# Dense attention scores: the 64-row products of two pairs of key tiles in the two halves of the array's rows

## The chip, the cores and the metric

The kernel runs on one core of one Trainium2 chip. The metric is device time in microseconds (us), lower is better; the median of three runs of the kernel before is 1220.64 us (1220.6 to 1221.4).

## The reference

One encoder layer over 1024 positions of width 1024, all in float32: RMS norm, one projection, two attention mixers side by side, an output projection, and a gated MLP with a three-wide convolution. The change lies in the first mixer, dense attention with 8 query heads and 2 key/value heads of width 64:

```python
def global_gqa_attention(q, k, v):
    ...
    def block(qb):
        sc = jnp.einsum('bqkgd,bskd->bkgqs', qb, k, preferred_element_type=jnp.float32) * scale
        p = jax.nn.softmax(sc, axis=-1)
        return jnp.einsum('bkgqs,bskd->bqkgd', p.astype(v.dtype), v)
```

## The kernel before

To keep float32 accuracy, operands are split into a high part of a shorter float and a low rest, and a product is the sum of three products: high by high, high by low, low by high. The head width is 64, and TensorE contracts over 128 rows, so the scores of one key tile take two matmuls. The arrays have the contraction on the rows (partitions):

- `q2` (`R_Q2A`, two buffers by the group's parity): rows 0 to 63 the high part of four heads' queries, rows 64 to 127 the low part; 512 columns.
- `R_K2A`: rows 0 to 63 the low part of the keys, rows 64 to 127 the high part. By `q2` it gives low by high plus high by low in one matmul (L773).
- `R_KHA`: rows 0 to 63 the high part of the keys, copied there by a DMA; rows 64 to 127 zero. By `q2` it gives high by high (L774), with half of the rows multiplying zeros.

The work is cut into 16 groups `g` (a block of 128 query positions by the four heads of one key/value head). `a_main_bounded` runs over four pairs `j` of key tiles; a pair is 2 tiles of 128 keys and fills two PSUM banks: 0 and 1 for even `j`, 2 and 3 for odd. For each pair TensorE does four score matmuls, ScalarE (ACT) takes the exponential of the two banks (L779) into one of three buffers, ACT (VectorE, that is DVE, for `j` = 1) makes the high part of it (L783, L781), and DVE the low part (L784). Three pairs later `pv` (L757) multiplies with the values, six matmuls a pair. At the end of a group DVE copies the sum out of PSUM (L767), TensorE transposes it (L762), and DVE divides (L803, L804).

Between these runs side work: `a_prep(g + 1)` prepares the next group's queries: `nat` splits them (L665 on ACT, L666 on DVE), `first` transposes them on TensorE (L192) and copies them to `q2` (L687 on ACT). The tuple `plan` tells at which key tile `kt` (two in each pair) the next of these steps is taken. Norm and rotary work of the late query heads (L530 and the eight L304 on GpSimd, that is POOL; some on DVE) and the first head of the second mixer (`b_split`, `b_prep`) are dealt out in the same way.

A scheduler takes the program in the order written and sets each engine's own order, by its estimate of when operands are ready; engines run their own list in order. POOL's list holds tensor operations and POOL's DMAs in one line. After the stage comes the second, dilated mixer, whose first score matmuls (L986) follow directly.

Of the kernel before, what the change touches and what calls it, by code (L numbers as in the profile page):

```python
# [45 lines left out]
R_K2A = 16384  # L46
R_KHA = R_K2A + 2048
R_W = R_KHA + 6144
# [26 lines left out]
R_QLN = R_XT + 1024  # L75
R_Q2A = R_XT + 2048
R_QLA = R_XT + 3072
R_PH = R_XT + 4096
R_PL = R_XT + 6144
R_VB = R_XT + 8192  # L80
# [56 lines left out]
def tile_encoder_layer(ctx, tc, x, w_in, gains, outg, norm1_g, norm2_g, w_out, w_up, conv_w, conv_b,  # L137
# [14 lines left out]
    def emit(bounded):  # L152
# [3 lines left out]
        gp = nc.gpsimd  # L156
        mm = nc.tensor.matmul
# [5 lines left out]
        def r(off, n):  # L163
            return bigr[:, off:off + n]
# [20 lines left out]
        def bank(i, n=512, o=0):  # L185
            return PS[:, 512 * i + o:512 * i + o + n]
# [485 lines left out]
        def a_prep(g):  # L672
            b, kv = grp(g)
            o = 512 * (g % 2)
            q2 = R_Q2A + 512 * (g % 2)
            ql = R_QLA + 512 * (g % 2)

            def nat():
                if bounded:
                    return q_pair(qab(b) + 256 * kv, 64, vec, 4, o)  # L680
                q_nat(qab(b) + 256 * kv, 64, vec, 4, o)

            def first():
                t = next_tr()
                for i in range(4):
                    tr_r(t, i, r(R_QD + o + 128 * i, 128))
                act(r(q2, 512), bank(t), AF.Copy)  # L687

            def mx(i):
                for hf in range(2):  # L690
                    b = hf
                    mm(bank(b), r(q2 + 128 * i, 128), r(R_K2A + 1024 * kv + 512 * hf, 512), start=True, stop=True)
                    vec.tensor_reduce(f(SM_MC + 8 * hf + i, 1), bank(b), axis=AX.X, op=OP.max)

            def last():
                vec.tensor_tensor(rp(R_QLN + 512 * kv + 64, [128, 4]), f(SM_MC, 4), f(SM_MC + 8, 4), op=OP.max)
                t = next_tr()
                for i in range(4):
                    tr_r(t, i, r(R_QLN + 128 * (4 * kv + i), 128))
                act(r(ql, 512), bank(t), AF.Copy)  # L700

            if bounded:
                return [nat, first]
            return [nat, first] + [lambda i=i: mx(i) for i in range(4)] + [last]
# [38 lines left out]
        def a_main_bounded(g, prep, tail, late, plan, late_plan):  # L743

            b, kv = grp(g)
            b2, kv2 = grp(max(g - 2, 0))
            q2 = R_Q2A + 512 * (g % 2)
            ob = 6 + g % 2
            slots = {}

            def pv(j):
                ph, pl = slots[j]
                for u in range(2):
                    kt = 2 * j + u
                    v = R_VA + 132 * kt + 66 * kv
                    for i, (w, p) in enumerate(((v, ph), (v + 1056, ph), (v, pl))):
                        mm(bank(ob)[0:66], r(w, 66), r(p + 512 * u, 512), start=(kt == 0 and i == 0), stop=(kt == 7 and i == 2))  # L757

            def o_turn():
                t = next_tr()  # L760
                for i in range(4):
                    nc.tensor.transpose(bank(t, 66, 128 * i), f(F_OT + 128 * i, 128)[0:66], f(O_IDF, 66)[0:66])  # L762
                o_norm(t, 128, qab(b) + 256 * kv, ([64, 4], [1, 64]))

            def last():
                pv(3)
                vec.tensor_copy(f(F_OT, 512)[0:66], bank(ob)[0:66])  # L767

            for j in range(4):
                st = 2 * (j % 2)  # L770
                for u in range(2):
                    kt = 2 * j + u
                    mm(bank(st + u), r(R_K2A + 1024 * kv + 128 * kt, 128), r(q2, 512), start=True, stop=False)  # L773
                    mm(bank(st + u), r(R_KHA + 1024 * kv + 128 * kt, 128), r(q2, 512), start=False, stop=True)  # L774
                n = pairs[0]
                pairs[0] += 1
                p, ph, pl = F_PB[n % 3], R_PHB[j], R_PLB[j]
                slots[j] = ph, pl
                act(f(p, 1024), bank(st, 1024), AF.Exp)  # L779
                if j == 1:  # L780
                    vec.tensor_copy(r(ph, 1024), f(p, 1024))  # L781
                else:
                    act(r(ph, 1024), f(p, 1024), AF.Copy)  # L783
                vec.tensor_tensor(r(pl, 1024), f(p, 1024), rf(ph, 1024), op=OP.subtract)  # L784
                for kt in (2 * j, 2 * j + 1):
                    take(prep, plan[kt])
                    take(late, late_plan[kt])
                    now = f(qab(b2) + 256 * kv2, 1) if 0 < kt < 7 and g > 1 else \
                        rf(R_Q2A + 512 * ((g + (kt == 7)) % 2), 1)
                    for step in spread.pop((g, kt), []):  # L790
                        step(now)
                step = tail.pop(0) if tail else None
                if step:
                    step()
                if j > 2:
                    pv(j - 3)

            behind, turn[:] = turn[:], [o_turn]
            return [lambda: [t() for t in [lambda: pv(1)] + behind], lambda: pv(2), last, o_turn if g == 15 else None]
# [550 lines left out]
        for g in range(16):  # L1350

            prep += a_prep(g + 1) if g < 15 else []
            if g == 14:
                prep += [lambda: b_split(0)] + sum(sum(b_prep(0), []), [])
            plan = {14: (1, 1, 0, 1, 0, 1, 1, 0), 15: (1, 1, 0, 1, 0, 0, 0, 0)}.get(g, (0, 1, 0, 0, 1, 0, 0, 0)) if bounded else {14: (1, 1, 1, 1, 1, 2, 2, 2), 15: (2, 2, 2, 2, 1, 1, 1, 1)}.get(
                g, (1, 1, 1, 1, 1, 1, 1, 0))
            tail = a_main(g, prep, tail, late, plan, (0, 2, 2, 2, 1, 1, 1, 1))
            if g == 7:
                if not bounded:
                    dma(f(F_CNT, 384), cnt)  # L1360
                if not bounded:
                    gp.memset(fp(F_VCN + 64, [66, 8]), 1.0)
                    load_vc(0)
            if g in (4, 7):
                wo_load(g // 7)
            if g == 9:
                load_tee(0, 0)
                load_tee(0, 1)
                load_tmx(1)
            if g == 11:  # L1370
                load_k(0)
            if g == 13:
                load_k(1)
            if g == 10 and bounded:
                load_v(0)
            if g == (12 if bounded else 5):
                v_split(R_VB, F_VBN)
                load_v(1)
            if g > 3 and fills:
                b, kv = grp(g - 2 if bounded else g - 1)  # L1380
                fills.pop(0)(qab(b) + 256 * kv)
# [411 lines left out]
        for m in range(2, len(order)):  # L1793
            j, n = order[m]
# [111 lines left out]
```

## Time and profile before

| what | value |
|---|---|
| median of the runs | 1220.64 us |
| the profiled execution, its own time | 1221.38 us |
| span of its trace | 1219.6 us |
| the stage of dense attention (16 groups), in the trace | 207.5 to 364.8 us |
| score matmuls in it (L773 and L774) | 128 and 128 |
| pairs of key tiles (16 groups of 4) | 64 |

Times inside the trace are counted from the start of the span. PE is TensorE's matmul row, PEld its weight loads. A matmul's row starts when it is issued and its end is modelled, so that rows of back-to-back matmuls overlap: what one costs in a stream is the distance from start to start. In a table by windows the columns are the window, its length, the busy time of PE, PEld, DVE, ACT and POOL with the number of instructions, the granted TensorE clock (1.00 is full), the share of DMA and GB/s.

### The profile page before, as it was taken

How to read it: one execution, taken by the hardware profiler on the slowest of the kernel's cores; microseconds unless marked ns; L12 is line 12 of the kernel's file. 1: busy time of each engine (PE TensorE's matmuls, PEld its weight loads, DVE VectorE, ACT ScalarE, POOL GpSimd, SP SyncE). 2: the span in 40 equal slices, each digit the busy share in tenths (PEclk: the TensorE clock that was granted, in tenths of full speed). 3: DMA queues.
4: the chain of work that ended last, by engine and by line, in shares of the span. 5: the costliest groups of instructions: out<-in, count | busy, mean ns of one | idle time of the engine just before them, and what ended most of it. 6: DMA issues, size and time to landing. Idle time of an engine off the chain costs nothing.

```text
span 1219.6 us, 17814 instructions
## 1 busy us (share of the span) xinstructions
PE 1191.7 (98%) x6615; PEld 1007.2 (83%) x6615; DVE 998.0 (82%) x1324; ACT 674.1 (55%) x976; POOL 398.4 (33%) x307
## 2 busy tenths in 40 slices
PE   7999999999999999999999999999999999999998
PEld 7999999666669997888788888877888788888886
DVE  5988687989988878666999999999999997876673
ACT  7856455889887767436544444445444453543431
POOL 1710122230024530010465666557575644000000
PEclk9999999999999999999999999999999999999999
DMA  8036301020015655232132232322332257977872
GB/s 281 25 103 154 108 18 42 1 57 18 1 30 125 153 117 173 89 102 95 61 112 95 87 113 97 111 95 87 113 112 100 83 184 252 338 239 243 291 233 85
DMA packets 121565, 147.00 MB, mean 121 GB/s; under 512 B 51137, under 2 KB 79617, under 8 KB 121473
## 3 DMA queue, kind: packets, MB, share of 16 engines
q1 hardware_dynamic: 119329, 140.05, 35.9%
q0 software_dynamic: 2144, 5.77, 2.2%
q8 instruction: 53, 0.87, 0.3%
q14 instruction: 39, 0.32, 0.1%
HBM read 107.25 MB, written 33.82 MB: 116 GB/s over the span
## 4 chain that ended last, share of the span: by engine, by line
PE 68%; DVE 17%; issue 5%; ACT 4%; DMA 3%; POOL 1%; SPq 0%; DVEq 0%; ACTq 0%; POOLq 0%
DVE bigf L1603 7%; PE ps L1570 7%; PE ps L1572 6%; PE ps L1571 6%; PE ps L757 6%; PE ps L1704 6%; PE ps L1703 6%; PE ps L1702 6%; DVE bigf L1574 3%; PE ps L1125 2%; PE ps L1126 2%; PE ps L1124 2%; PE ps L434 2%; PE ps L435 2%; PE ps L773 2%
## 5 line engine op out<-in xcount | busy, mean ns | idle before, releaser
L1570 PE MATMUL ps<-bigr 128*128 128x512 f32 x616 | 241.0, 392 | 6.3 <-DVE bigf L1574 5.8
L1571 PE MATMUL ps<-bigr 128*128 128x512 f32 x616 | 239.7, 389 | 0.0
L1572 PE MATMUL ps<-bigr 128*128 128x512 f32 x616 | 239.7, 389 | 0.0
L1603 DVE SCALAR_TENSOR_TENSOR bigf<-bigf 128x768 f32<-128x768 f32 (+1 forms) x176 | 178.7, 1073 | 26.5 <-ACT bigf L1601 26.4
L1553 ACT ACTIVATE bigr<-bigf 128x512 fp32r<-128x512 f32 x154 | 93.2, 625 | 139.5 <-POOL bigf L1545 70.2
L1682 ACT ACTIVATE bigr<-bigf 128x1024 fp32r<-128x1024 f32 (+1 forms) x99 | 83.7, 867 | 115.8 <-PE ps L1704 67.6
L1570 PEld LDWEIGHTS ps<-bigr 128*128 128x128 f32 x616 | 115.6, 188 | 35.0 <-DVE bigf L1574 9.2
L1572 PEld LDWEIGHTS ps<-bigr 128*128 128x128 f32 x616 | 115.6, 188 | 24.1
L1571 PEld LDWEIGHTS ps<-bigr 128*128 128x128 f32 x616 | 115.7, 188 | 23.7
L434 PE MATMUL ps<-bigr 128*128 128x256 f32 x448 | 127.3, 285 | 1.2 <-ACT bigf L310 1.2
L1554 DVE TENSOR_TENSOR bigr<-bigf,bigr 128x512 fp32r<-128x512 f32 x112 | 125.2, 1135 | 3.2 <-ACT bigr L1553 2.5
L435 PE MATMUL ps<-bigr 128*128 128x256 f32 x448 | 126.9, 283 | 0.6 <-DVE bigr L418 0.6
L436 PE MATMUL ps<-bigr 128*128 128x256 f32 x448 | 126.7, 283 | 0.0
L1702 PE MATMUL ps<-bigr 128*128 128x512 f32 x308 | 119.8, 389 | 0.0
L1703 PE MATMUL ps<-bigr 128*128 128x512 f32 x308 | 119.8, 389 | 0.0
L1704 PE MATMUL ps<-bigr 128*128 128x512 f32 x308 | 119.8, 389 | 0.0
L1683 DVE TENSOR_TENSOR bigr<-bigf,bigr 128x1024 fp32r<-128x1024 f32 (+1 forms) x99 | 97.6, 1005 | 24.8 <-ACT bigr L1682 21.4
L757 PE MATMUL ps<-bigr 128*66 128x512 f32 x384 | 99.9, 394 | 0.0
L434 PEld LDWEIGHTS ps<-bigr 128*128 128x128 f32 x448 | 85.8, 192 | 1.8 <-ACT bigf L310 1.5
L435 PEld LDWEIGHTS ps<-bigr 128*128 128x128 f32 x448 | 85.9, 192 | 0.8 <-DVE bigr L418 0.8
L784 DVE TENSOR_TENSOR bigr<-bigf,bigr 128x1024 fp32r<-128x1024 f32 x64 | 80.8, 1269 | 6.4 <-ACT bigr L783 5.7
L436 PEld LDWEIGHTS ps<-bigr 128*128 128x128 f32 x448 | 85.9, 192 | 0.0
(231 smaller groups left out, 2508.8 us busy)
## 6 DMA issues: line engine op xcount, KB each, us to landing
bigf<-w_down SPq DMA_DIRECT2D x99, 256.0 KB, 4.3
bigf<-w_up SPq DMA_DIRECT2D x44, 512.0 KB, 3.6
bigf<-gscr SPq DMA_DIRECT2D x77, 256.0 KB, 4.3
gscr<-bigf SPq DMA_DIRECT2D x31, 512.0 KB, 2.6
bigf<-w_in SPq DMA_DIRECT2D x8, 1024.0 KB, 5.4
bigf<-x SPq DMA_DIRECT2D x15, 512.0 KB, 7.0
bigf<-w_out SPq DMA_DIRECT2D x8, 512.0 KB, 3.9
bigr<-bigr POOLq DMA_DIRECT2D x16, 256.0 KB, 3.8
```

Source lines behind the costliest of these rows:

```text
L434: mm(o, ah, wh, start=(k == 0 and t % 2 == 0 and n != 2), stop=False, skip_group_check=True)
L435: mm(o, ah, wl, start=False, stop=False, skip_group_check=True)
L436: mm(o, al, wh, start=False, stop=(k == 3), skip_group_check=True)
L757: mm(bank(ob)[0:66], r(w, 66), r(p + 512 * u, 512), start=(kt == 0 and i == 0), stop=(kt == 7 and i == 2))
L1554: (gp if n in (2, 4) and m > 3 else vec).tensor_tensor(rp(o + 512, [128, 4], [1, 128]), src, rfp(o, [128, 4], [1, 128]), op=OP.subtract)
L1570: mm(bank(b), wh, th, start=(k == 0 and n in (1, 5, 6, 7)), stop=False, skip_group_check=True)
L1571: mm(bank(b), wh, tl, start=False, stop=False, skip_group_check=True)
L1572: mm(bank(b), wl, th, start=False, stop=(k == 3), skip_group_check=True)
L1603: vec.scalar_tensor_tensor(f(a + o, n), f(i + d, n), w_, f(a + o, n), op0=OP.mult, op1=OP.add)
L1702: mm(o, ah, r(d, 512), start=(q == 0 and n in (1, 5, 2)), stop=False, skip_group_check=True)
L1703: mm(o, ah, r(d + 1024, 512), start=False, stop=False, skip_group_check=True)
L1704: mm(o, al, r(d, 512), start=False, stop=(q == NQ - 1), skip_group_check=True)
```

## The change

Every pair still takes its two L773 matmuls over 128 rows. The high-by-high products, which need 64 rows only, become 64-row matmuls: for the first key tile of a pair from rows 0 to 63 (`R_KHA` by `q2`), for the second from rows 64 to 127 (the high keys in the lower half of `R_K2A`, by a copy of the high queries at rows 64 to 127, `R_Q3A`). They write two different banks. So that two pairs' 64-row matmuls stand together, those of pair `j` (even) and pair `j + 1` are both issued at pair `j`: there they are the last products into pair `j`'s banks and the first ones into pair `j + 1`'s, to which the 128-row matmuls are added later. The copy `R_Q3A` is made for each group by a DMA on POOL's queue (64 rows by 512 columns, 128 KB), after the query copy. The tuple `plan` takes the query preparation one pair earlier.

```diff
+R_Q3A = R_W + 6144
...
                 act(r(q2, 512), bank(t), AF.Copy)
+                if bounded:
+                    gp.dma_start(r(R_Q3A + 512 * (g % 2), 512)[64:128], r(q2, 512)[0:64])
...
                 for u in range(2):
-                    kt = 2 * j + u
-                    mm(bank(st + u), r(R_K2A + 1024 * kv + 128 * kt, 128), r(q2, 512), start=True, stop=False)
-                    mm(bank(st + u), r(R_KHA + 1024 * kv + 128 * kt, 128), r(q2, 512), start=False, stop=True)
+                    mm(bank(st + u), r(R_K2A + 1024 * kv + 256 * j + 128 * u, 128), r(q2, 512), start=j % 2 == 0, stop=j % 2 == 1)
+                for i in (j, j + 1) if j % 2 == 0 else ():
+                    k2, kh = [o + 1024 * kv + 256 * i for o in (R_K2A, R_KHA)]
+                    for lo, k, q in ((0, kh, q2), (64, k2 + 128, R_Q3A + 512 * (g % 2))):
+                        mm(bank(2 * (i % 2) + lo // 64), r(k, 128)[lo:lo + 64], r(q, 512)[lo:lo + 64], start=i != j, stop=i == j)
...
-            plan = {14: (1, 1, 0, 1, 0, 1, 1, 0), 15: (1, 1, 0, 1, 0, 0, 0, 0)}.get(g, (0, 1, 0, 0, 1, 0, 0, 0)) if bounded else ...
+            plan = {14: (1, 0, 1, 0, 1, 1, 1, 0), 15: (1, 1, 0, 1, 0, 0, 0, 0)}.get(g, (0, 1, 1, 0, 0, 0, 0, 0)) if bounded else ...
```

Lines below L690 stand five further down in the changed kernel: L773 is L775, the 64-row matmuls are L779, L757 is L760, L192 is L193, L687 is L688, the new DMA is L690, L779 (the exponential) is L784, L783 is L788, L530 and L304 are L531 and L305, L838 is L843.

TensorE's list in the middle of a group, before. Two pairs of four score matmuls, with the next group's query transposes (L192) and the six value matmuls (L757) between them:

```order
L773 MATMUL ps<-bigr 128x512 [waits Activation_49]
L774 MATMUL ps<-bigr 128x512
L773 MATMUL ps<-bigr 128x512
L774 MATMUL ps<-bigr 128x512
L192 MATMUL ps<-bigr 128x128 x4
L757 MATMUL ps<-bigr 66x512 x2
L757 MATMUL ps<-bigr 66x512 [waits DVE_49]
L757 MATMUL ps<-bigr 66x512 x3
L773 MATMUL ps<-bigr 128x512 [waits Activation_49]
```

And with the change, an odd pair and the even one after it:

```order
L775 MATMUL ps<-bigr 128x512 x2
L193 MATMUL ps<-bigr 128x128 x4
L760 MATMUL ps<-bigr 66x512 x2
L760 MATMUL ps<-bigr 66x512 [waits DVE_49]
L760 MATMUL ps<-bigr 66x512 x3
L775 MATMUL ps<-bigr 128x512 [waits Activation_49]
L775 MATMUL ps<-bigr 128x512
L779 MATMUL ps<-bigr 128x512 x2
L779 MATMUL ps<-bigr 128x512 [waits Activation_49]
L779 MATMUL ps<-bigr 128x512
L760 MATMUL ps<-bigr 66x512 x2
```

The odd pair has two score matmuls left; the even one has two over 128 rows and then four over 64, and the third of these, which opens the next pair's banks, waits for ACT's exponential of the pair before. There are 128 matmuls L779 in the stage, in 35 unbroken stretches.

POOL's list in groups 0 to 4, before:

```order
L304 TENSOR_TENSOR bigf<-bigf 128x8x16 x5
L530 TENSOR_TENSOR bigf<-bigf 128x512 [waits DVE_49,Pool_49]
L304 TENSOR_TENSOR bigf<-bigf 128x8x16 [waits Pool_49]
L304 TENSOR_TENSOR bigf<-bigf 128x8x16 x7
L530 TENSOR_TENSOR bigf<-bigf 128x512 [waits DVE_49,Pool_49]
L304 TENSOR_TENSOR bigf<-bigf 128x8x16 [waits Pool_49]
L304 TENSOR_TENSOR bigf<-bigf 128x8x16 x7
L1452 MEMSET bigf 128x8
```

And with the change:

```order
L305 TENSOR_TENSOR bigf<-bigf 128x8x16 x5
L690 DMA bigr<-bigr 64x512 [waits Activation_49]
L690 DMA bigr<-bigr 64x512 [waits DMASW4_49,Activation_49]
L690 DMA bigr<-bigr 64x512 [waits DMASW5_49,Activation_49]
L531 TENSOR_TENSOR bigf<-bigf 128x512 [waits DVE_49,Pool_49]
L305 TENSOR_TENSOR bigf<-bigf 128x8x16 [waits Pool_49]
L305 TENSOR_TENSOR bigf<-bigf 128x8x16 x7
L690 DMA bigr<-bigr 64x512 [waits DMASW6_49,DMASW0_49,Activation_49]
L531 TENSOR_TENSOR bigf<-bigf 128x512 [waits DVE_49,Pool_49]
L305 TENSOR_TENSOR bigf<-bigf 128x8x16 [waits Pool_49]
L305 TENSOR_TENSOR bigf<-bigf 128x8x16 x7
L1457 MEMSET bigf 128x8
```

The copies of the queries of groups 1 to 3 stand ahead of the second rotary batch, that of group 4 between the second and the third, and that of group 5 behind the third and the MEMSET.

ACT's list around the second GpSimd split (L838), before, with one query copy (L687):

```order
L779 ACTIVATE bigf<-ps 128x1024 [waits DVE_49,PE_49] x2
L687 ACTIVATE bigr<-ps 128x512 [waits PE_49]
L783 ACTIVATE bigr<-bigf 128x1024 [waits Activation_49]
L838 ACTIVATE bigr<-bigf 128x8x64 [waits DMAHW6_49,DMAHW5_49,DMAHW7_49,DMAHW4_49,PE_49]
L779 ACTIVATE bigf<-ps 128x1024 [waits DVE_49,PE_49]
```

And with the change:

```order
L784 ACTIVATE bigf<-ps 128x1024 [waits DVE_49,PE_49]
L688 ACTIVATE bigr<-ps 128x512 [waits DMASW7_49,PE_49]
L784 ACTIVATE bigf<-ps 128x1024 [waits DVE_49,PE_49]
L788 ACTIVATE bigr<-bigf 128x1024 [waits Activation_49]
L843 ACTIVATE bigr<-bigf 128x8x64 [waits DMAHW6_49,DMAHW5_49,DMAHW7_49,DMAHW4_49,PE_49]
L784 ACTIVATE bigf<-ps 128x1024 [waits DVE_49,PE_49]
```

The query copy stands one exponential earlier, and waits for an earlier one of the new DMAs as well, which read the same buffer.

More of the change, by code (lines that the diff above doesn't have):

```diff
@@ L1354, in emit @@
                 prep += [lambda: b_split(0)] + sum(sum(b_prep(0), []), [])
-            plan = {14: (1, 1, 0, 1, 0, 1, 1, 0), 15: (1, 1, 0, 1, 0, 0, 0, 0)}.get(g, (0, 1, 0, 0, 1, 0, 0, 0)) if bounded else {14: (1, 1, 1, 1, 1, 2, 2, 2), 15: (2, 2, 2, 2, 1, 1, 1, 1)}.get(
+            plan = {14: (1, 0, 1, 0, 1, 1, 1, 0), 15: (1, 1, 0, 1, 0, 0, 0, 0)}.get(g, (0, 1, 1, 0, 0, 0, 0, 0)) if bounded else {14: (1, 1, 1, 1, 1, 2, 2, 2), 15: (2, 2, 2, 2, 1, 1, 1, 1)}.get(
                 g, (1, 1, 1, 1, 1, 1, 1, 0))
```

## Prediction

> **What bounds the kernel now.** I read the page's busy times first, then the chain of waits, then the stage of dense attention by windows of one group each, then the rows of single matmuls. The page:
>
> ```profile
> span 1219.6 us, 17814 instructions
> PE 1191.7 (98%) x6615; PEld 1007.2 (83%) x6615; DVE 998.0 (82%) x1324; ACT 674.1 (55%) x976; POOL 398.4 (33%) x307
> PE 68%; DVE 17%; issue 5%; ACT 4%; DMA 3%; POOL 1%; SPq 0%; DVEq 0%; ACTq 0%; POOLq 0%
> ```
>
> Over the whole span TensorE is the bound, and the chain that ended last runs 68% through it. But an average says nothing of one stage. Here are the 16 groups, a window each (columns: window, length, busy PE, PEld, DVE, ACT, POOL, clock, DMA share, GB/s):
>
> ```profile
> 207.50:213.00 5.50, 5.24 (x28) 3.93 (x26) 3.89 (x5) 4.66 (x7) 0.00 (x0) 1.00 0.00 0
> 213.00:223.30 10.30, 10.29 (x44) 6.94 (x45) 10.30 (x13) 9.55 (x12) 0.00 (x0) 1.00 0.00 0
> 223.30:233.20 9.90, 9.90 (x50) 6.87 (x49) 8.49 (x14) 8.02 (x11) 4.11 (x4) 1.00 0.01 2
> 233.20:243.00 9.80, 9.80 (x50) 6.80 (x48) 9.24 (x13) 7.82 (x10) 3.65 (x6) 1.00 0.00 1
> 243.00:252.90 9.90, 9.90 (x50) 6.88 (x49) 7.39 (x14) 7.92 (x10) 7.25 (x10) 1.00 0.19 47
> 252.90:264.20 11.30, 10.00 (x49) 6.73 (x48) 10.61 (x16) 8.38 (x11) 3.10 (x1) 1.00 0.36 88
> 264.20:274.10 9.90, 9.90 (x50) 6.89 (x49) 9.42 (x17) 9.26 (x13) 1.39 (x1) 1.00 0.11 27
> 274.10:283.90 9.80, 9.80 (x49) 6.72 (x48) 9.74 (x16) 9.70 (x12) 0.00 (x0) 1.00 0.19 54
> 283.90:293.80 9.90, 9.90 (x50) 6.89 (x50) 9.60 (x19) 8.78 (x11) 0.00 (x0) 1.00 0.01 2
> 293.80:303.90 10.10, 10.10 (x51) 6.77 (x49) 9.53 (x15) 9.50 (x13) 0.00 (x0) 1.00 0.00 0
> 303.90:313.60 9.70, 9.70 (x48) 6.81 (x48) 8.90 (x16) 9.66 (x12) 0.00 (x0) 1.00 0.01 2
> 313.60:323.50 9.90, 9.90 (x50) 6.86 (x49) 9.62 (x17) 8.06 (x10) 0.00 (x0) 1.00 0.00 1
> 323.50:333.30 9.80, 9.80 (x49) 6.80 (x48) 9.56 (x15) 7.83 (x9) 0.00 (x0) 1.00 0.00 0
> 333.30:343.10 9.80, 9.80 (x49) 6.86 (x48) 9.70 (x18) 8.30 (x12) 0.00 (x0) 1.00 0.13 28
> 343.10:354.70 11.60, 10.75 (x58) 7.49 (x57) 8.71 (x13) 10.05 (x14) 1.42 (x1) 1.00 0.00 1
> 354.70:364.80 10.10, 10.10 (x54) 7.15 (x53) 7.63 (x8) 9.60 (x14) 4.68 (x5) 1.00 0.27 54
> ```
>
> PE is busy without a gap in most groups, at the full clock. But DVE is close behind: 9.74 of 9.80 us in group 7 (the eighth row), all of group 1, over 95% in most of groups 7 to 13; ACT is at 9.70 and 9.66 in groups 7 and 10. So what TensorE saves in a group comes out only as far as the busier of the other two allows. The stage is 157.3 us (first to last window), and the dilated stage follows on PE at once, so a shift here reaches the end.
>
> The price of a matmul is read from start to start:
>
> ```profile
> 264.24 0.40 PE L773 MATMUL ps<-bigr 128*128 128x512 f32 x1
> 264.24 0.19 PEld L774 LDWEIGHTS ps<-bigr 128*128 128x128 f32 x1
> 264.47 0.39 PE L774 MATMUL ps<-bigr 128*128 128x512 f32 x1
> 264.70 0.39 PE L773 MATMUL ps<-bigr 128*128 128x512 f32 x1
> 264.93 0.40 PE L774 MATMUL ps<-bigr 128*128 128x512 f32 x1
> 265.16 1.54 PE L757 MATMUL ps<-bigr 128*66 128x512 f32 x6
> 266.54 0.41 PE L762 MATMUL ps<-bigf 66*128 66x66 f32 x4
> 266.75 0.48 PE L773 MATMUL ps<-bigr 128*128 128x512 f32 x1
> 267.07 0.39 PE L774 MATMUL ps<-bigr 128*128 128x512 f32 x1
> 270.04 0.46 PE L192 MATMUL ps<-bigr 128*128 128x128 f32 x4
> 270.34 1.59 PE L757 MATMUL ps<-bigr 128*66 128x512 f32 x6
> ```
>
> 0.23 us each, and the six of L757 take 1.38. The weights of the next matmul load while one streams (the PEld row starts with it). The row's length, 0.39, is 0.16 more than 0.23: the modelled way through the array.
>
> **The change, part by part.** *Fewer streams.* 128 half-empty matmuls become 64 side-by-side couples if the halves run together: 64 x 0.23 = 14.7 us less on PE.
>
> *A ramp.* The second half of a stretch cannot start before its own weights are there. Four L192 with four weight loads take 0.30 us (270.04 to 270.34), so a load takes at most 0.075. In 35 stretches that is 2.6 us back.
>
> [...]
>
> *Changing the array's shape.* 35 stretches mean 70 changes. No row has one; L593's single 8-row matmul tells nothing. Lower bound 0: L774 to L757 changes the number of columns at no cost. Nearest row: after the transposes L762 the matmul after the first comes 0.32 us on (266.75 to 267.07) and not 0.23, 0.09 more. Upper bound: each change waits for the way through the array and for a weight load that was not fetched ahead, 0.16 + 0.19 = 0.35. I take 0.09, since a change of the array's use is what that row shows: 70 x 0.09 = 6.3 us. PE's net saving is 14.7 - 2.6 - 6.3 = 5.8 us, 0.36 a group.
>
> *What the others let through.* For each group the smaller of 0.36 and the window less the larger of DVE and ACT: 0.36 in groups 0, 2 to 6, 9, 14 and 15 (nine, 3.24 us), and 0 (group 1), 0.06 (7), 0.30 (8), 0.04 (10), 0.28 (11), 0.24 (12), 0.10 (13). Sum 4.3 us.
>
> *An earlier wait.* At an even pair the third 64-row matmul opens the next pair's banks, so it needs the exponential of the pair before one turn earlier. From that pair's last score matmul there are now six L757, two 128-row matmuls and one couple, 1.38 + 0.46 + 0.23 = 2.1 us; before it was four score matmuls and twelve L757, 3.7. Queued behind the wait are one more 64-row matmul and the six L757; ACT keeps work meanwhile. In group 6:
>
> ```profile
> 272.45 0.39 PE L774 MATMUL ps<-bigr 128*128 128x512 f32 x1
> 274.92 1.03 ACT L779 ACTIVATE bigf<-ps 128x1024 f32<-128x1024 f32 x1
> ```
>
> The exponential of an odd pair ended at 275.95, 3.1 us after its scores (272.84): 1.0 too late. That is a group with a whole extra L1074 on ACT; at 95% ACT or more (groups 1, 7, 9, 10) I expect such a wait about once in two, 0.6 us each after PE's slack of 0.36: an estimate of 1.2 us. Bounds: nothing, and 1.0 in each of 16 groups.
>
> *The copy by DMA.*
>
> ```profile
> 262.23 0.59 ACT L687 ACTIVATE bigr<-ps 128x512 fp32r<-128x512 f32 x1
> bigr<-bigr POOLq DMA_DIRECT2D x4, 128.0 KB, 2.6
> bigr<-bigr POOLq DMA_DIRECT2D x16, 256.0 KB, 3.8
> 246.58 4.72 POOL L304 TENSOR_TENSOR bigf<-bigf 128x128 f32<-128x128 f32 x8
> 252.87 0.39 PE L773 MATMUL ps<-bigr 128*128 128x512 f32 x1
> 358.28 1.23 DVE L784 TENSOR_TENSOR bigr<-bigf,bigr 128x1024 fp32r<-128x1024 f32 x1 [2.37 <-ACT bigr L783]
> 359.03 0.52 POOL L880 DMA_DIRECT2D bigr<-bigr  x1 [0.84 <-ACT bigr L876]
> ```
>
> The query copy ended 1.4 us before the next group (262.82 to 264.24); one pair earlier (2.3 us) makes 3.7, and the copied half is first needed 0.5 later, at 4.2. A POOL transfer of the same size lands in 2.6, twice the size in 3.8. So it is hidden, by 1.6 us, and what it costs beyond that is paid in every group. One is not: group 5's copy stands behind the third rotary batch, which ended at 251.30; 2.6 more is 253.9, and group 5 needs it at 252.87 + 0.46 + about 0.1. I count 0.4 us. Its issue (0.52 on POOL) does not stretch DVE: L784 took 1.23 with one beside it. SP's list is unchanged.
>
> *Sum.* 1221.38 (the profiled execution, 1.78 outside its span) - 4.3 + 1.2 + 0.4 = 1218.7. The median of the runs shown is 0.74 below that execution, so **1217.9 us**; rivals below carry the same 0.74.
>
> **The rivals.**
>
> *Each change drains the array.* 70 x 0.16 = 11.2 us leave PE 0.9 of its 12.1, and the waits (1.6) are no longer covered: 1220.64 - 0.9 + 1.6 = 1221.3. For it: overlapping rows mean there is work in flight to wait for. Against: L762 to L773 shows 0.09 only. It decides from about 0.15 a change.
> [...]
>
> *Drain and a fresh weight load* (the other side): 0.35 x 70 = 24.5 against 12.1, so PE needs 12.4 more; its idle time in the stage, 2.4 us by the windows (157.30 less 154.89), takes that much: 1220.64 + 10.0 = 1230.6. For it: both halves' weights belong to another shape. Against: all loads in the trace run ahead.
>
> *The halves run in turn*, so the change does not do what it says: nothing saved, 6.3 for the changes and 1.6 of waits, less 2.4: 1226.1. For it: no row has two matmuls streaming at once, starts are never nearer than a stream. Against: they share neither rows nor banks.
>
> *The copy is late in every group.* It decides from 4.2 us after the query copy. Landing at 4.8 costs 0.6 in 15 groups, 9.0 less the 4.3 gained: 1225.3. For it: the 3.8 of the larger POOL DMA. Against: 2.6 at the same size.
>
> *Changes are free and nothing waits*: PE saves 12.1, 0.75 a group; by the windows 0.75 in groups 0, 2, 4 and 14, else what the larger neighbour leaves (0.56, 0.69, 0.48, 0.06, 0.30, 0.57, 0.04, 0.28, 0.24, 0.10, 0.50), 6.1 in all: 1214.5.
>
> **How the numbers follow.** My forecast 41%, with its own range 1215.5 to 1219.8; drain 18%, drain and load 13%, in turn 9%, late copy 9%, free 10%. What a measurement of this kernel tells from no change is 0.2%, 2.4 us: faster is below 1218.2, slower above 1223.1. The forecast lies near that line: 30 of its 41 points are faster, 11 no change. The drain: 2 faster, 8 no change, 8 slower. Free is faster; the other three are slower. Faster 42%, same 19%, slower 39%. The range leaves out half of drain and load and a little of free: 1213 to 1230.
>
> **What would show it.** Right: second halves starting well under 0.23 us after first ones; the L757 after a stretch within 0.1 us of its usual place; groups 2 to 6 about 0.36 us shorter, groups 7 to 13 near DVE's busy time. The drain: gaps of 0.16 or more on both sides of each stretch. In turn: four 64-row matmuls 0.23 apart. The late copy: PE waiting for a DMA at each group's second 64-row matmul. ACT late: waits for the exponential at the third. Wrong altogether: a stage longer than 157.3 us, or changed elsewhere than in this stage.

## The result, and the profile after

The change made the kernel slower by a little: 1223.58 us (median of 20 runs, 1222.07 to 1226.59) against 1220.75 us for the kernel before beside it (20 runs, 1219.14 to 1222.87). The ratio is 1.0023, 95% interval 1.0016 to 1.003, just over the 0.2% that the prediction takes for a difference. The forecast was 1217.9 us and faster. The time lies inside the wide range of 1213 to 1230, but outside the forecast's own 1215.5 to 1219.8, and the sign is the other one. The profiled execution took 1222.45 us, with a span of 1220.6.

The page of the kernel after, its span, busy times and chain:

```profile
span 1220.6 us, 17863 instructions
PE 1191.7 (98%) x6615; PEld 992.2 (81%) x6615; DVE 997.6 (82%) x1324; ACT 675.5 (55%) x976; POOL 407.9 (33%) x323
PE 69%; DVE 16%; issue 5%; ACT 4%; DMA 3%; POOL 2%; SPq 0%; DVEq 0%; ACTq 0%; POOLq 0%
```

Nothing of the change can be read here: PE is busy for 1191.7 us, to the tenth what it was, for "busy" holds PE's slow stretches too (2.00 of 2.00 us at a clock of 0.50, in group 5 below). The stage of dense attention has to be opened. The groups of the kernel after, a window each (columns: window, length, busy PE, PEld, DVE, ACT, POOL, clock, DMA share, GB/s):

```profile
212.70:223.70 11.00, 11.00 (x45) 5.96 (x46) 10.40 (x13) 9.52 (x12) 0.51 (x1) 1.00 0.13 24
223.70:233.30 9.60, 9.60 (x50) 5.77 (x49) 9.12 (x14) 8.26 (x11) 4.13 (x4) 1.00 0.08 15
252.60:266.00 13.40, 11.59 (x50) 6.55 (x48) 12.10 (x19) 9.27 (x12) 3.65 (x6) 0.87 0.41 94
266.00:275.70 9.70, 9.70 (x50) 5.83 (x49) 8.24 (x18) 9.62 (x13) 2.34 (x2) 1.00 0.19 41
305.00:314.70 9.70, 9.70 (x50) 5.93 (x50) 9.15 (x13) 9.28 (x11) 0.51 (x1) 1.00 0.08 15
333.90:343.50 9.60, 9.60 (x50) 5.78 (x49) 9.36 (x16) 8.35 (x12) 0.51 (x1) 1.00 0.20 44
343.50:355.80 12.30, 10.58 (x58) 6.42 (x57) 8.45 (x12) 9.82 (x14) 2.61 (x2) 1.00 0.06 11
```

These are groups 1, 2, 5, 6, 10, 13 and 14. Most groups (here 2, 6, 10 and 13) became shorter, by about 0.2 us. Three became longer: group 1 from 10.3 to 11.0, group 5 from 11.3 to 13.4, group 14 from 11.6 to 12.3. Group 5 is also the only one with a granted clock below 1.00 (0.87).

Measured exactly, from the start of a group's first 128-row score product to that of the next:

| us | 1 | a regular group | 5 | 6 | 7 | 14 | 15 | stage |
|---|---|---|---|---|---|---|---|---|
| before | 10.31 | 9.85 | 11.37 | 9.83 | 9.86 | 11.53 | 10.10 | 157.2 |
| after | 10.99 | 9.63 | 13.44 | 9.65 | 9.95 | 12.26 | 9.92 | 158.5 |

So the stage gained about 0.2 us in each regular group and lost 0.7 + 2.1 + 0.7 us in three others: together +1.3 us. The stages behind it kept their lengths, 208.7 and 646.2 us before, 209.0 and 645.9 after, so this was not passed on or made up elsewhere.

**A stretch of 64-row products.** Weight loads and products in group 6 of the kernel after, in order of start:

```profile
266.00 0.63 PE L775 MATMUL ps<-bigr 128*128 128x512 f32 x2
266.56 0.30 PEld L779 LDWEIGHTS ps<-bigr 64*128 64x128 f32 x4 [0.37 <-issue]
266.56 0.74 PE L779 MATMUL ps<-bigr 64*128 64x512 f32 x4
267.22 1.12 PEld L760 LDWEIGHTS ps<-bigr 128*66 128x66 f32 x6 [0.37 <-issue]
267.22 1.59 PE L760 MATMUL ps<-bigr 128*66 128x512 f32 x6
```

The two halves do run at once: four products of L779 take 0.66 us from their start to the next line's, where four 128-row products took 0.92 before, and within a couple the second starts 3 ns after the first. But the two L775 take 0.56 to the first L779, 0.10 more than 2 x 0.23; the couples take 0.66, 0.20 more than 2 x 0.23; and the first L760 to the second takes 0.28, 0.05 more. That is 0.35 us of overhead per stretch, against 0.46 saved. The PEld rows show what goes with it: the weights of the first couple and of the first L760 are no longer loaded while the products ahead of them stream, but start with their own product, behind an idle 0.37 that nothing but "issue" ends. In the kernel before the load of L774 ran beside L773 (both from 264.24).

In these rows a change of shape stops the flow, weight loads included (PEld idle for 0.37 us on either side); in and out together cost about 0.35 us. Whether the array empties, or the weights merely come late, or both, the rows do not separate.

**Group 5.** PE and POOL there:

```profile
247.41 5.70 POOL L305 TENSOR_TENSOR bigf<-bigf 128x128 f32<-128x128 f32 x8
253.09 0.57 POOL L690 DMA_DIRECT2D bigr<-bigr  x1
253.12 0.49 PE L779 MATMUL ps<-bigr 64*128 64x512 f32 x1
255.43 1.04 PE L779 MATMUL ps<-bigr 64*128 64x512 f32 x3 [1.81 <-DMA bigr<-bigr]
256.40 2.82 PE L760 MATMUL ps<-bigr 128*66 128x512 f32 x6
```

POOL's third rotary batch ended 0.5 us into the group and not ahead of it; the copy of the queries was issued at 253.09 and landed at 255.4; PE waited 1.81 us for it. Then six L760 took 2.8 us and not 1.4. The granted clock says why (columns: window, length, busy PE, clock, DMA share, GB/s):

```profile
252.00:254.00 2.00, 1.61 (x7) 1.00 0.00 0
254.00:256.00 2.00, 0.57 (x3) 0.92 0.58 120
256.00:258.00 2.00, 2.00 (x7) 0.50 0.34 77
258.00:260.00 2.00, 2.00 (x12) 0.73 0.39 92
```

After the wait the clock fell to 0.50 for 3.4 us, about half of which is lost to PE (an estimate from that clock). A second such spell stands late in the dilated stage of this profile:

```profile
462.00:464.00 2.00, 0.78 (x11) 0.97 0.54 221
464.00:466.00 2.00, 2.00 (x13) 0.50 0.03 8
466.00:468.00 2.00, 2.00 (x16) 0.68 0.42 98
```

The profile of the kernel before has neither. The second is not the change's own, though: the kernel before with one tick moved (experiment 6) shows a fall at the same place (a clock of 0.92 from 460 to 464 us and 0.66 from 464 to 468).

**Group 14, and the waits of the stage.** PE's waits in groups 5 to 7 and in group 14 of the kernel before (columns: engine and line, what it waited for, us in total, times, the longest), then PE in group 14 of the kernel after, and then rows of its list of waits over the whole stage:

```profile
PE ps L762 <- DVE bigf L767: 1.3, 1, 1.3
PE ps L192 <- POOL bigr L666: 0.8, 1, 0.8
```
```profile
354.66 0.54 PE L193 MATMUL ps<-bigr 128*128 128x128 f32 x4 [1.72 <-POOL bigr L667]
```
```profile
PEld ps L779 <- issue: 12.4, 34, 0.4
PEld ps L760 <- issue: 10.8, 32, 0.7
POOL bigf L531 <- DVE bigf L1328: 6.8, 1, 6.8
PE ps L779 <- DMA bigr<-bigr: 1.8, 1, 1.8
DVE bigf L538 <- POOL bigf L305: 1.6, 1, 1.6
PEld ps L779 <- ACT bigf L784: 0.4, 2, 0.2
```

The wait for the exponential that the prediction priced at 1.2 us came to 0.4 us of PEld's time here, twice in the stage; experiments 1 and 4 show it larger. The wait for a DMA came once, in group 5 only. In group 14 PE's wait for the next queries grew from 0.8 to 1.7 us.

### The profile page after: what moved, and what is told of

Read it like the earlier page. It is cut to its first block, busy times and chain, and to the rows that moved or that the text cites. A ratio compares the mean times of both kernels' runs of the same rounds, so it can differ in the third digit from the quotient of the medians.

```text
span 1220.6 us, 17863 instructions
## 1 busy us (share of the span) xinstructions
PE 1191.7 (98%) x6615; PEld 992.2 (81%) x6615; DVE 997.6 (82%) x1324; ACT 675.5 (55%) x976; POOL 407.9 (33%) x323
## 4 chain that ended last, share of the span: by engine, by line
PE 69%; DVE 16%; issue 5%; ACT 4%; DMA 3%; POOL 2%; SPq 0%; DVEq 0%; ACTq 0%; POOLq 0%
PE ps L760 7%; PE ps L1575 7%; PE ps L1576 6%; PE ps L1577 6%; DVE bigf L1608 6%; PE ps L1708 6%; PE ps L1707 6%; PE ps L1709 6%; DVE bigf L1579 2%; PE ps L1129 2%; PE ps L1131 2%; PE ps L1130 2%; PE ps L775 2%; PE ps L435 2%; PE ps L436 2%
## 5 line engine op out<-in xcount | busy, mean ns | idle before, releaser
L760 PE MATMUL ps<-bigr 128*66 128x512 f32 x384 | 103.4, 402 | 0.0
L789 DVE TENSOR_TENSOR bigr<-bigf,bigr 128x1024 fp32r<-128x1024 f32 x64 | 81.4, 1282 | 12.2 <-ACT bigr L788 11.9
```

## The experiments

Theory, from these traces: the couples gain about 0.2 us a group, and side work eats it: the copy of group 5 on POOL, the new plan of group 14, the split stretch of group 1. Rivals: the 64-row shape itself costs the time; or the reordered products do, whatever their shape.

**1. The copy on SP's queue.**

```diff
-                    gp.dma_start(r(R_Q3A + 512 * (g % 2), 512)[64:128], r(q2, 512)[0:64])
+                    dma(rf(R_Q3A + 512 * (g % 2), 512)[64:128], rf(q2, 512)[0:64])
```

> The change, with the query copy's DMA issued from SP's queue in place of POOL's; nothing else differs in the source. Theory A (the loss is a few waits: the copy of group 5 stuck behind POOL's rotary batch, with the clock falling to half after it, 2.1 us in that group): the wait for the DMA and the fall of the clock are gone, group 5 is back near 11.2 us from 13.4, the median falls by about 2.3 us, to about 1221.3. Theory B (the changes of the array's shape eat the saving in every group and the waits only show up where there was slack anyway): the time stays within 0.7 us of 1223.6.

Measured: 1222.19 us (11 runs), ratio 1.0011 (1.0002 to 1.002), 1.4 us below the change. Group 5 fell to 11.14, but 6 and 7 grew to 10.82 and 10.45. What stood behind the copy came forward:

```profile
ACT bigr L854 <- DMA bigf<-kscr: 2.6, 1, 2.6
```

ACT's split of a dilated key tile, put into group 5 by the scheduler, waited for its load. In the change the same split had its data by the time that ACT came to it, because PE was late already. So removing one stall uncovered part of a second. PE itself waited for ACT: 2.1 us in three places at the third 64-row product, the one that opens the next pair's banks and needs an earlier exponential.

**2. The old plan of group 14**, alone and with SP's copy.

```diff
-            plan = {14: (1, 0, 1, 0, 1, 1, 1, 0), ...
+            plan = {14: (1, 1, 0, 1, 0, 1, 1, 0), ...
```

> The change with the plan of group 14 put back to what it was (POOL still copies). If the loss lies in side work (group 14's plan 0.7, group 5's copy about 2.1 with the half clock behind it) and the couples themselves gain 0.2 per group: group 14 goes from 12.26 to about 10.0 to 11.5, group 5 stays near 13.4, the regular groups stay at 9.6, median 1221.5 to 1222.5 against 1223.6. If the plan is innocent: 1223.6, group 14 stays at 12.3.

> As the run before, and with the plan of group 14 as it was before the change (1, 1, 0, 1, 0, 1, 1, 0). Theory A: group 14 falls from 12.3 to about 11.3 us too (it was 11.5 before the change), so about 0.8 us less than the run before, 1220.4, which is level with the kernel before or a little faster. Theory B: group 14 gets shorter and the groups around it longer, 1223.

Measured: 1221.16 us alone, ratio 1.0004 (0.9995 to 1.0013), and 1221.02 with SP's copy, ratio 1.0001 (0.9992 to 1.001). Group 14 fell to 9.95 and 15 rose to 11.31: 21.26 for both, after 22.18 in the change and 21.63 before. That is 0.9 us by the groups, but 2.4 us by the medians. The rest may be the clock's: the 20 runs of the change have a mean granted clock of 0.996 in most (12 runs), those of this kernel 0.998 or 0.999 in all. One spell of 3.4 us at 0.50 is worth 0.0014 of the mean, so by estimate the difference is one to two spells a run. One was caught in experiment 1, where PE's wait for L667 in group 14 was followed by 0.50. But in the profiled execution of the change the same wait of 1.72 us was followed by none, and the kernel of experiment 4, which has the new plan too, ran at 0.998 to 1.000: how the spells hang on the plan is not shown.

**3. Each pair has its own couple**, four stretches a group in place of two (65 unbroken ones in its trace in place of 35). The odd pairs' banks are then no longer opened a pair ahead; plan and copies are those of the change.

```diff
-                    mm(bank(st + u), ..., start=j % 2 == 0, stop=j % 2 == 1)
-                for i in (j, j + 1) if j % 2 == 0 else ():
+                    mm(bank(st + u), ..., start=True, stop=False)
+                for i in (j,):
```

> The change, but every pair takes its own 64-row matmuls (two a stretch, 64 stretches in place of 35), so the number of changes of the array's shape nearly doubles and the earlier wait for the exponential is gone. From the rows of the changed kernel a stretch has 0.095 + 0.106 + 0.097 + 0.05 us beside its two couples; a stretch of one couple has 0.095 + 0.097 + 0.05 = 0.24. Theory A: no saving is left on PE (0.23 saved, 0.24 paid), a regular group takes about 9.85 us, and the median is about 2.5 us above the change, 1226. Theory B': if the price is the wait for the exponential and not the shape, the groups get shorter than 9.63 us and the median is at or below 1223.

Measured: 1228.69 us, ratio 1.0061 (1.0046 to 1.0077), regular groups 10.3 and not 9.85. A group has four couples either way, so its products save the same 0.92; the two stretches more cost 0.67, that is 0.34 each. This measures the overhead of a stretch by its number, and agrees with the 0.35 read from the starts. The expectation was 0.24 and 1226 us: it took the 0.10 between two couples for something that a lone couple does not pay. A lone couple pays it too: it takes 0.43 us from its first start to the next line's, again 0.20 more than 0.23. The weights are late in each of them:

```profile
PEld ps L779 <- issue: 23.7, 65, 0.4
```

**4. The same order and plan with 128-row products.** The couples run as the four 128-row products of the kernel before; nothing is left out. The copies by POOL's DMA are still made, but nothing reads them.

> The change's order, plan and DMA, but with 128-row matmuls in place of the 64-row ones (the zero rows back, both by the same queries, the copied queries unread). It prices the shape alone. Theory A: regular groups take 9.85 us as in the kernel before (PE saves nothing), no wait for the copy, clock full; the order and plan alone cost group 14 0.7 us: median about 1221.5. Theory B: the time is below 1220, as all of the loss is the shape's.

Measured: 1222.36 us, ratio 1.0011 (1.0002 to 1.0021). Regular groups 9.81, group 1 10.23, groups 5 to 7 10.81, 11.02, 10.45, group 14 12.28. So the order, the plan and the unread copies cost about 1.5 us against the kernel before, with no 64-row product in the program. The long groups 5 to 7 and 14 are theirs; group 1's extra 0.7 and most of the 0.2 gained in a regular group (9.81 to 9.63; the other 0.04 is the order's) belong to the couples. PE's only wait in groups 5 to 7 of this kernel:

```profile
PE ps L779 <- ACT bigf L784: 1.8, 3, 0.8
```

That is the wait for an earlier exponential again, now ahead of a 128-row product (L779 in this kernel): it comes with the order and not with the shape. It shows in every kernel of the new order in which no copy is late for PE in group 5 (1.3 to 2.2 us of PE's time there), in none in which one is late, and not in experiment 3, whose banks are not opened ahead. There groups 5 to 7 take 10.76, 10.37 and 10.33, near the other groups' 10.3, though PE is slower in that kernel and leaves ACT more time.

**5. The key load held back**, so that the split of experiment 1 no longer waits: with SP's copy and the old plan, in the kernel before alone, and with POOL's copy and the old plan.

```diff
+                if bounded:
+                    hold(F_KN[0], f(qab(grp(9)[0]) + 256 * grp(9)[1], 1))
```

> The change with the copy on SP's queue, group 14's plan as before, and the load of dilated key tile 0 (and so ACT's split of it, L854) held until the queries of group 9 stand in the registers, so that ACT no longer waits for that load in the middle of groups 5 to 7. If that wait (2.7 us in the run with the first two edits) is what eats the gain: groups 6 and 7 fall from 10.8 and 10.5 to 9.6, group 5 to 9.7 to 10.5, median 1217.5 to 1219.0. If groups 5 to 7 are late for another reason (the queue, the rotary batch on POOL): they stay, median 1221.0. If the dilated mixer then starts late because its first split is late: the groups fall but the later part grows, median 1219.5 to 1221.

> The kernel before with the same hold on the load of dilated key tile 0 and nothing else: what the hold is worth without the change. By the wait theory group 5 goes from 11.37 to about 9.9 and the rest stays: median 1219.2 to 1219.8. If the hold is what makes the last kernel fast, this one gains as much as that. If the hold delays the dilated mixer: 1220.8 or above.

> The last but one with the copy left to POOL: what the copy's place alone costs when neither group 14's plan nor the split's load is in the way. If the copy of group 5 waits behind POOL's third rotary batch as it does in the change: group 5 near 13 (with a half clock spell behind it), median 1.5 to 3 above the kernel with SP's copy (1219.5 to 1221.5). If the rotary batch itself was late through the hoisted split: group 5 falls too and the two kernels are within 0.5 us.

Measured: 1220.49 us (ratio 0.9997, 0.9988 to 1.0006); 1220.76 (1.0, 0.9991 to 1.0009); 1221.81 (1.001, 1.0001 to 1.0019). The wait for the load was gone, but groups 5 to 7 took 10.62, 10.81, 10.46, hardly less than the 11.18, 10.83, 10.48 with it: the theory that this wait costs 2 us fell. Likewise group 5 of the kernel before stayed at 11.31. In group 5 something else ended last, and group 6 was then full on ACT (rows of the waits of the first of the three, then groups 5 and 6 of it, columns as above):

```profile
ACT bigf L563 <- DVE bigf L559: 2.7, 1, 2.7
DVE bigf L538 <- POOL bigf L305: 1.6, 1, 1.6
```
```profile
253.34:263.96 10.62, 10.02 (x49) 5.52 (x48) 10.00 (x15) 6.82 (x9) 0.60 (x3) 1.00 0.35 82
263.96:274.77 10.81, 9.97 (x48) 5.97 (x49) 9.49 (x18) 10.75 (x15) 1.81 (x1) 1.00 0.16 36
```

DVE waits for POOL's third batch, ACT's square L563 for DVE, and the exponentials stand behind L563 on ACT, which is idle for 2.7 us in group 5 and busy for 10.75 of 10.81 in group 6, with 15 operations where the kernel before has 13: some of what group 5 did not take runs there. PE waits for the exponentials at the end of this chain, 1.3 us in two places at the third 64-row product and 0.6 at an L775. With the copy on POOL group 5 was 13.49, as in the change, so that is a price of the copy's place: 1.3 us between the two medians.

**6. POOL's third batch started earlier**: its tick on DVE two key tiles ahead, with SP's copy and the old plan, in the kernel before alone, and with POOL's copy and the old plan.

```diff
-..., (third, ((3, 6), (4, 4), (4, 6)))):
-                spread[at[0]] = tick + run(ts[:5])
+..., (third, ((3, 4), (4, 4), (4, 6)))):
+                spread[at[0]] = spread.get(at[0], []) + tick + run(ts[:5])
```

> The change with the copy on SP's queue, group 14's plan as before, and the DVE tick that lets POOL start the third rotary batch (L1328) moved from key tile 6 of group 3 to key tile 4, so that it stands one low part (L789) earlier in DVE's order. In the run with the hold POOL's batch ended at 253.83 and DVE's L538 had waited 1.6 for it, and ACT's L563 2.7 for DVE, though nothing waited for the key load any more. If that chain (late tick, late batch, late DVE, late ACT) is what makes groups 5 to 7 long: their sum falls from 31.9 to 32.5 to between 29.5 and 30.7, median 1218.3 to 1219.5. If groups 5 to 7 are long because of the reordered products themselves: they stay at 32 and the median at 1220.5 to 1221.

> The kernel before with the same tick moved and nothing else; it moves one place in DVE's order, past the copy of 66 rows. By the chain theory group 5 of the kernel before (11.37) falls by the 0.7 of that copy at most: median 1220.0 to 1220.8. If the tick alone is worth what the last kernel gains: 1219.5 or below.

> As the first, with the copy left to POOL. By the chain theory the copy of group 5 is issued about 1.8 earlier and PE waits for it some 0.3 in place of 2.1; no half clock follows: group 5 near 11, median 1219.0 to 1220.0. If the copy on POOL has a price of its own in every group: 0.5 to 1.5 above the first.

Measured: 1220.33 us (ratio 1.0, 0.9991 to 1.001); 1220.46 (1.0, 0.999 to 1.0009); 1221.55 (1.0005, 0.9996 to 1.0014). Group 5 was 10.87, 11.36 and 13.19. The edit missed its aim, so the chain theory was not tested by it. POOL in the first of them, and the DVE operation beside it:

```profile
245.22 2.74 POOL L531 TENSOR_TENSOR bigf<-bigf 128x512 f32<-128x512 f32 x1 [5.77 <-DVE bigf L1328]
245.60 1.21 DVE L789 TENSOR_TENSOR bigr<-bigf,bigr 128x1024 fp32r<-128x1024 f32 x1
248.04 5.68 POOL L305 TENSOR_TENSOR bigf<-bigf 128x128 f32<-128x128 f32 x8
```

L531 started earlier, but took 2.74 us where the change shows 1.28, so the batch ended 0.2 us into group 5 in place of 0.5. In the change it was the DVE operation beside L531 that took long:

```profile
246.04 1.28 POOL L531 TENSOR_TENSOR bigf<-bigf 128x512 f32<-128x512 f32 x1 [6.76 <-DVE bigf L1328]
246.19 2.23 DVE L789 TENSOR_TENSOR bigr<-bigf,bigr 128x1024 fp32r<-128x1024 f32 x1 [0.30 <-ACT bigr L788]
```

L789 takes 1.2 us elsewhere. In each case one of the two keeps its usual time and the other takes 1.0 to 1.5 us longer. In the change DVE's row begins 0.14 us after POOL's and DVE is the long one. In the first kernel here POOL's row begins 0.38 us ahead of DVE's and POOL is the long one, so the order of the recorded starts does not decide it; why one of them is long is not shown. Here the earlier start on POOL came with a longer run, 2.74 us.

**7. What the halves are worth with every other edit equal**: the first kernel of experiment 6 with the couples as 128-row products, as in experiment 4.

> As the first, with the products of the couples run as 128-row products again (the first two of the couple, of the same keys and queries, over all 128 rows, so four more terms of the same kind in place of the halves): what the halves alone are worth with every other edit equal. Regular groups 9.81 against 9.62: 13 x 0.19 = 2.5 longer than the first if the halves gain what the regular groups show; the same as the first, within 0.5, if DVE or ACT sets the length of the groups.

Measured: 1221.94 us, ratio 1.0012 (1.0003 to 1.0021), against 1220.33 with the halves in the same set of runs: the halves gain 1.6 us by the medians (2.5 were expected), 1.0 by the stages of the two profiled executions (157.8 and 156.8). Their regular groups are 0.2 shorter (9.63 against 9.81), their group 1 is 0.7 longer (10.96 against 10.23). Groups 5 to 7 take 32.07 and 32.13: nothing is gained there.

**8. Two losses by themselves.** On top of the first kernel of experiment 5: the waiting DVE operations of the third batch put later (with the earlier tick of experiment 6); the couples of group 1 as 128-row products; and both.

```diff
-..., (third, ((3, 6), (4, 4), (4, 6)))):
+..., (third, ((3, 4), (4, 6), (5, 2)))):
```
```diff
+                        if g == 1:
+                            mm(bank(2 * (i % 2) + lo // 64), r(kh + 2 * lo, 128), r(q2, 512), start=i != j, stop=i == j)
+                            continue
```

> The kernel with SP's copy, the old plan of group 14 and the hold, and in it the DVE operations that consume POOL's third rotary batch put later (L538 from key tile 4 of group 4 to 6, L541 from key tile 6 of group 4 to key tile 2 of group 5) and the tick at key tile 4 of group 3. If DVE's 1.6 us wait for POOL and ACT's 2.7 us wait behind it make groups 5 to 7 long: their sum falls from 31.9 to 30 to 31, median 1219.3 to 1220.0 against 1220.5. If not: 31.9 and 1220.5.

> The kernel with SP's copy, the old plan of group 14 and the hold, with the couples of group 1 alone as the 128-row products of the kernel before. If group 1's loss is the split couple (a half by itself, products of 66 columns, the other half): group 1 falls from 10.99 to about 10.25, all else the same, median 1219.8. If it is the reordered work of the head of the stage: it stays at 10.9.

> Both edits at once: if they add up and the waits are what costs, group 1 at 10.25 and groups 5 to 7 at 30 to 31, median 1218.7 to 1219.4, below the kernel before (1220.6). If only group 1's part holds: 1219.8.

Measured: 1220.04 us (ratio 0.9993, 0.9984 to 1.0002), 1219.66 (0.9997, 0.9988 to 1.0006) and 1219.35 (0.9993, 0.9984 to 1.0002). In the first and the third the square of key tile 2 in group 5 takes the entry of the table to which the add was moved, so the add of the third batch (L541, 1.2 us of DVE) is left out: their times do not tell what an order with the add would give. In them groups 5 to 7 fell from 31.89 to 30.98 while DVE's wait for POOL stayed:

```profile
DVE bigf L538 <- POOL bigf L305: 1.6, 1, 1.6
ACT bigf L563 <- DVE bigf L559: 0.8, 1, 0.8
PE ps L779 <- DMA bigr<-bigr: 1.1, 1, 1.1
```

With 1.2 us less on DVE ahead of it, ACT's wait fell from 2.7 to 0.8 and group 6 to 9.61; group 5 was longer, 11.16, with a new wait of PE for the copy, and PE no longer waited for an exponential. That fits the chain from DVE to ACT to PE, but does not show that the chain alone makes up the loss.

The edit of group 1 did what it should: 10.24 and not 10.99, the rest as before. The couple there had been torn apart; PE in group 1 of the change, and of the kernel with this edit (L780 is its 128-row product in group 1):

```profile
213.33 0.50 PE L779 MATMUL ps<-bigr 64*128 64x512 f32 x1
213.76 1.38 PE L760 MATMUL ps<-bigr 128*66 128x512 f32 x5
215.07 0.50 PE L779 MATMUL ps<-bigr 64*128 64x512 f32 x1
215.50 0.68 PE L760 MATMUL ps<-bigr 128*66 128x512 f32 x2
216.11 0.50 PE L779 MATMUL ps<-bigr 64*128 64x512 f32 x2
```
```profile
212.87 0.62 PE L780 MATMUL ps<-bigr 128*128 128x512 f32 x2
213.33 1.79 PE L760 MATMUL ps<-bigr 128*66 128x512 f32 x7
214.96 0.62 PE L780 MATMUL ps<-bigr 128*128 128x512 f32 x2
```

The scheduler drew a half, a half and a couple apart with L760 between them: one stretch became three, and two halves ran alone. Three streams of 0.23 and three visits of 0.35 make 1.74 us where four 128-row products take 0.92. That is 0.82 more, less the 0.11 that the group's other stretch saves: 0.71, and 0.75 was measured.

No kernel of these that computes everything is measurably faster than the kernel before. The nearest, with SP's copy, the old plan, the hold and 128-row products in group 1, has a median 0.8 us below it, and an interval that holds 1.

## Why the prediction was wrong

Two steps failed. The change of the array's shape was priced at 0.255 us a stretch and costs 0.35, so that PE's net saving is less than half of the 5.8 us forecast. And the side work of the new order was priced at 0.4 us for one late copy, where groups 1, 5 and 14 lose 3.5 us.

**The halves run at once: right.** Each couple saves a stream of 0.23 us; the rival of halves in turn is out, by the starts 3 ns apart.

**The price of a change of shape: the term that was too small.** The sum took a ramp of 0.075 and twice 0.09 a stretch, 0.255; the starts give 0.35 and experiment 3 gives 0.34. That is 0.175 a change. By size it is nearest to the rival in which each change drains the array (0.16 a change, 11.2 us in all; measured 35 x 0.35 = 12.3); by the weights that come late it is the other rival, at half its price of 0.35 a change. The gaps lie 0.10 ahead of the first couple, 0.10 behind it, 0.10 behind the last one and 0.05 after that, not 0.16 on both sides, so neither rival holds as it was put, and no run tells the drain from the late load. The prediction took the 0.09 of the transposes for a change of shape. At the transposes the next weights still begin ahead of their product (266.72 and 266.75 in the kernel before), and here they do not. A regular group has two stretches, 0.92 - 0.70 = 0.22 us saved; measured 0.22 (9.85 to 9.63), of which the order alone gave 0.04 (experiment 4). The net saving of PE was to be 5.8 us and is about 14.7 - 35 x 0.35 = 2.5 us. Between the halves of a couple the rows show no ramp: 3 ns from start to start.

**What DVE and ACT let through: too little in the groups where they looked full.** Group 13 was to gain 0.10 and group 10 0.04; they gained 0.23 and 0.09. DVE's busy time there fell with the group's length (in group 13 from 9.70 us in 18 operations to 9.36 in 16), so what looked like a full engine did not hold the group at its length. This term did not decide the sign. (The rival with free changes adds up to 6.8 us by its own terms, 1213.8, and not to 6.1.)

**The earlier wait for the exponential: the mechanism was right, the place was not.** 1.2 us was priced, for groups 1, 7, 9 and 10, said to have ACT at 95% or more; by the table groups 1 and 9 are at 93% and 94%. In the change 0.4 us is there. But there PE was late already, behind the copy in group 5, and ACT waited for it (up to 2.6 us at once). In the kernels without that stall PE waits 1.3 to 2.2 us for the exponentials, all in groups 5 to 7, where ACT is first held up by DVE or by a load and then full.

**The copy by DMA: right in its place, wrong in its size.** Only group 5 waits, as said, and for the reason said. The term was 0.4 us; PE waited 1.81, and the group lost 2.1. The prediction took the end of POOL's batch from the trace before, 1.6 us ahead of the group. In the new order DVE's tick L1328 comes later, POOL's batch ends 0.5 us into the group, and the transfer takes another 2.3 (the 2.6 that was priced was enough).

**What had no term.** The new plan of group 14, 0.9 us by the groups and 2.4 by the medians, 1.2 with SP's copy beside it (experiment 2). The torn couple of group 1, 0.7 us. Groups 5 to 7, in which the new order costs about a microsecond even without the copy on POOL (31.9 to 32.5 against 31.1 before): PE waits there for the earlier exponential, and the chain of waits behind it was found, but no kernel of the new order that computes everything and is rid of it; what would remove it stays open. And the fall of the clock behind some of PE's stalls, which turns the wait of 1.81 us into a loss of up to 3.5, by an estimate from 3.4 us at 0.50.

**The sum as it came.** Groups 2 to 4 and 6 to 13: 2.0 us gained. Groups 1, 5, 14 and 15: 3.3 us lost. That is the stage's +1.3 in the profiled run, and +1.1 in its time (1222.45 after 1221.38); the median is 2.8 above. Its runs without a visible loss of clock (0.999 and 1.000) lie at 1222.07 to 1223.11, the twelve at 0.996 at 1222.45 to 1225.24, so some of the difference may be spells of lost clock that the profiled run has fewer of; how many each stall causes was not settled. So most of the miss lies where side work is: in groups 1, 5, 14 and 15 the forecast had 1.1 us let through less 0.4 for the copy, and 3.3 were lost. In all other groups together it had 3.2, and 2.0 came; the 1.2 for the exponential did not come in the change. The sign that the prediction named for being wrong altogether, a stage longer than 157.3 us, came (158.5).

## What to carry to other kernels

Two half-empty products side by side saved a stream of 0.23 us here, but a visit to the half-array shape cost about 0.35 us with one couple as with two: gather couples into long stretches, and keep a scheduler from drawing them apart. A saving of 0.2 us a group was smaller here than one wait of side work that the new order brought (1.81 us in group 5), so price the tables and queues that come with a change as carefully as the change itself, from the order of the kernel after. When a stall is removed and the time stays, look for the next one in the same place before doubting the first.

## What the runs showed of the hardware

- The clock fell to 0.50 for 3.4 us after PE had waited 1.81 us for the copy (group 5 of the change), to 0.50 after a wait of 1.75 us in group 14 of experiment 1's kernel, and to 0.50 for 3.4 us near 463 us of the change, after waits of 0.77 and 1.22 us that lay 1.5 us apart. It did not always follow such waits: the kernel before has waits of 0.76 and 1.23 us at the same place and shows no fall there, and none followed the 1.72 us wait in group 14 of the change.
- Weight loads began one product ahead within the streams of the kernel before (the load of L774 at 264.24, with L773, its own product at 264.47). In the change they did not cross from 128-row to 64-row products or back: 34 idle stretches of PEld ahead of L779 and 32 ahead of L760, 0.37 us in the group shown, where "issue" is all that the profile has for a reason. A visit to the 64-row shape cost 0.35 us with two couples and 0.34 with one (experiment 3).
- Of a POOL operation (L531) and a DVE operation (L789) that ran side by side, one took longer than elsewhere: POOL's 2.74 in place of 1.28 us in the first kernel of experiment 6, DVE's 2.23 in place of 1.2 in the change. Which of the two it is does not follow from the recorded starts alone.
